# A two-layer encoder kernel: gates weighed two units sooner, scores scaled in place by the instruction that takes their extremum, queries turned with tables that hold gain and angle

## The chip, the cores and the metric

The kernel runs on one NeuronCore of a Trainium2 chip. The metric is the device time of one execution in microseconds (us). The kernel before has a median of 2119.84 us over three runs (2119.44 to 2119.92). The engines are called PE (TensorE, matrix products; PEld is its weight load), DVE (VectorE), ACT (ScalarE), POOL (GpSimd) and SP (SyncE, which here only issues DMAs).

## The reference, cut to what matters

The program is an encoder of two layers over 512 tokens of width 2048: gated grouped-query attention, then gated retention, each followed by a layer norm. The change touches the attention layer alone. There are 16 query heads of 128 elements in 4 groups; each group shares one key and value head.

```
def rms_norm(x, gain):
    y = x32 * lax.rsqrt(jnp.mean(x32 * x32, axis=-1, keepdims=True) + RMS_EPS)
    return (y * gain).astype(x.dtype)

def apply_rope(x, cos, sin):
    a, b, c, d = jnp.split(x32, 4, axis=-1)
    rot = jnp.concatenate([-b, a, -d, c], axis=-1)
    return x32 * cos + rot * sin
...
    q = apply_rope(rms_norm(q, q_gain), cos, sin) * (A_HEAD_DIM ** -0.5)
    k = apply_rope(rms_norm(k, k_gain), cos, sin)
...
        s = jnp.einsum('bkgqd,bskd->bkgqs', qb, k)
        p = jax.nn.softmax(s, axis=-1)
        return jnp.einsum('bkgqs,bskd->bkgqd', p, v)
...
    return (o * jax.nn.silu(g)) @ w_out
```

## The kernel before

**Products.** Every float32 product is made of three matmuls of split operands (`mm3`, L267 to L269): high by high, high by low, low by high. A weight chunk of 128 x 1024 is loaded as `raw`; ACT casts its high half `whi` and DVE subtracts to get the low half `wlo` (`split`, L116). Chunks are split two ahead of their use (`AHEAD = 2`) and loaded three further ahead. The projections are made by a seven-product scheme of 2 x 2 blocks, so DVE also adds `raw` to `raw` (L186, L188) and operand quarters `xf` to `xf` (L312 to L318).

**Order.** The instructions of PE run in the order of the program text. Those of the other engines are put in order by a scheduler, which goes by what is ready and, among ready ones, by where they stand in the text. Each engine then runs its own list strictly in order and waits at semaphores.

**Queries and keys.** When a tile of 128 tokens of a query or key projection is complete, `deliver_1` hands it to `rotate`, a generator whose pieces run one by one at chunk starts (`run_later`): square (ACT, L683), times gain (DVE, L684), sum of squares (L689), reciprocal root on POOL (L504, into `q_rs` for queries), then the rotation in halves (L700, L703, L706, two of each). A key is also scaled by its reciprocal root (L710); a query is not, its `q_rs` is applied to the scores. Three chunks later `put` transposes the tile on PE (`r_dst`, L521) and stores it in DRAM. A stretch of the const pool, `tabs`, holds the gains, cosines and sines.

**Attention.** `attention` walks through units. A unit is one head `h` of one query tile `t` of one group `g`: 64 units in two calls of 32, which share PE with products of the projection (`work.pump`). At step `u` PE makes the scores of unit `u` (`scores`, 128 x 512 in a PSUM bank `s`); DVE takes their negated maximum (L772); ACT multiplies it by `q_rs` (L773) and takes the exponential with `q_rs` as scale and that product as bias (L775), with the row sum in `sm`. At step `u` also unit `u - 2` is turned (`turn`: four transposes `tr<-ident,p` on PE, split into `pTh` by ACT and `pTl` by DVE), and for every second unit the two heads up to unit `u - 4` are multiplied with the values (`values`, into `o`). After the last head of a tile `weigh` divides the tile's gate by the sums: a reciprocal on DVE (L789, `rs`) and a product on POOL (L791, `gate<-gate,rs`). `close` then transposes that gate on PE (`tr<-ident,gate`), and the product of both becomes an operand of the output projection.

Gates, queries, keys and values come back from DRAM by DMAs that SP issues (L750 to L762). POOL issues the accumulating weight loads (L144) and the stores, in one list with its arithmetic.

Of the kernel before, what the change touches and what calls it, by code (L numbers as in the profile page):

```python
# [13 lines left out]
P = 128  # L14
# [38 lines left out]
def encoder_trunk_kernel(  # L53
# [52 lines left out]
    def v4(x):  # L106
        return x.rearrange("p (n d) -> p n d", d=P)
# [569 lines left out]
        for i in range(2):  # L677
            hook(a_in[3], ORDER[t + 3 * i], 1 + i, residual_1, t, i)

    def rotate(t, qk, src, g, put):  # L680

        sq, x = temp("r_sq"), src
        nc.scalar.activation(sq, src, AF.Square)  # L683
        nc.vector.scalar_tensor_tensor(  # L684
            out=v4(x), in0=v4(src), scalar=P ** -0.5 if qk == 0 else 1.0,
            in1=gains[:, qk].unsqueeze(1).broadcast_to([P, 4, P]), op0=ALU.mult, op1=ALU.mult)
# [3 lines left out]
        if qk == 0:  # L690
            rs = q_rs[:, g, t]
        else:
            rs = small("k_rs", 4)
        rsqrt(rs, ss, 1.0 / P, RMS_EPS)
        yield
        dst = temp("r_dst")
        xv, tv, dv = [m.rearrange("p (n h i d) -> p n h i d", n=4, h=2, i=2) for m in (x, sq, dst)]
        cb, sb = [m[:, t].unsqueeze(1).broadcast_to([P, 4, 2, 32]) for m in (cos, sin)]
        for i in range(2):
            nc.vector.tensor_tensor(out=tv[:, :, :, i], in0=xv[:, :, :, 1 - i], in1=sb, op=ALU.mult)  # L700
            if i:
                yield
            nc.vector.tensor_tensor(out=dv[:, :, :, i], in0=xv[:, :, :, i], in1=cb, op=ALU.mult)  # L703
            if not i:
                yield
            nc.vector.tensor_tensor(out=dv[:, :, :, i], in0=dv[:, :, :, i], in1=tv[:, :, :, i],  # L706
                                    op=ALU.subtract if i == 0 else ALU.add)
        yield
        if qk:
            nc.vector.tensor_tensor(out=v4(dst), in0=v4(dst), in1=rs.unsqueeze(2).broadcast_to([P, 4, P]), op=ALU.mult)  # L710
        soon(3, put, dst)

    def deliver_1(blk, nb, t, src, own):
        kind, g = A_COLS[a_in.index(blk)][nb]
        if kind in "vg":
            o = src if own else temp("gt")
        if kind == "v":
            if not own:
                nc.scalar.copy(o, src)
            nc.gpsimd.dma_start(out=vD[:, t], in_=o)  # L720
        elif kind == "g":
            if blk is a_in[-1]:
                e = temp("e")
                nc.scalar.activation(e, src, AF.Tanh, scale=0.5)
                nc.vector.scalar_tensor_tensor(out=o, in0=e, scalar=1.0, in1=src, op0=ALU.add, op1=ALU.mult)
            else:
                nc.scalar.activation(o, src, AF.Silu)
            nc.gpsimd.dma_start(out=gD[g][:, t], in_=o)
        else:
            def put(m):  # L730
                o = temp("qkT")
                nc.scalar.copy(o, transpose4(m))
                stored.add((kind, g, t))
                if kind == "q":
                    nc.gpsimd.dma_start(out=qD[g][:, t], in_=o)
                else:
                    nc.gpsimd.dma_start(out=kD[:, :, tcols(t)], in_=v4(o))

            turn_soon(lambda t, src: rotate(t, 0 if kind == "q" else 1, src, g, put), t, src, own)

    class Group:
        def __init__(self, g, op=None):
            self.g, self.op, self.q, self.gate, self.ogs, self.pT, self.sm = g, op, {}, {}, {}, {}, {}
# [20 lines left out]
        def scores(self, t, h):  # L764
            sb = bank("s")
            q = self.q[t]
            mm3(sb, [half(q, i)[:, tcols(h)] for i in range(2)], [half(self.k, i) for i in range(2)], True, True)
            if h == 0:
                self.sm[t] = small("sm", 4)
            rs = q_rs[:, self.g, t, h:h + 1]  # L770
            nmax = small("nmax")
            nc.vector.tensor_reduce(out=nmax, in_=sb, axis=AX.X, op=ALU.max, negate=True)  # L772
            nc.scalar.mul(nmax, nmax, rs)  # L773
            pt = temp("p")
            nc.scalar.activation(pt, sb, AF.Exp, scale=rs, bias=nmax, accum_out=self.sm[t][:, h:h + 1])  # L775
# [8 lines left out]
        def weigh(self, t):  # L784

            rs, sm = small("rs", 4), self.sm.pop(t)
            if ("g", self.g) in A_COLS[-1]:
                nc.vector.tensor_scalar_mul(sm, sm, 2.0)
            nc.vector.reciprocal(rs, sm)  # L789
            gt = self.gate.pop(t)  # L790
            nc.gpsimd.tensor_tensor(out=v4(gt), in0=v4(gt), in1=rs.unsqueeze(2).broadcast_to([P, 4, P]), op=ALU.mult)  # L791
            self.gt = gt

        def values(self, t, hh):

# [6 lines left out]

        def close(self, t):
            gT = temp("gT")
            nc.scalar.copy(gT, transpose4(self.gt))
            if self.op:
                nc.vector.tensor_tensor(out=self.op.quarter(t // 2, self.g % 2)[:, :, tcols(t % 2)],
                                        in0=v4(self.ob), in1=v4(gT), op=ALU.mult)
                if t == 1:
                    self.op.form(1 + self.g % 2)  # L810
                return
            if t % 2 == 0:
                self.ogs[t // 2] = x4("ogh"), x4("ogl")
            nc.vector.tensor_tensor(out=gT, in0=self.ob, in1=gT, op=ALU.mult)
            split(*[half(m, t % 2) for m in self.ogs[t // 2]], gT)
# [4 lines left out]
    def attention(gs, nxt, work, pace):  # L820
# [4 lines left out]
        for u in range(len(units) + LOOK + 2):  # L825
            each = pace(u)
            if u < len(units):
                g, t, h = units[u]
                n = after[g]
                if h == 1:  # L830
                    if t + 2 < NT:
                        g.load_q(t + 2)
                    elif n:
                        if t + 2 == NT:
                            n.load_kv()
                        n.load_q(t + 2 - NT)
                if h == 2:
                    g.load_gate(t)
                p[u] = g.scores(t, h)
            work.pump(each / 2)  # L840
            w = u - LOOK
            if 0 <= w < len(units):
                g, t, h = units[w]
                g.turn(t, h, p.pop(w))
            w = u - LOOK - 2
            if w >= 0 and w % 2:
                g, t, h = units[w]
                g.values(t, h // 2)
                if h == HPG - 1:
                    g.weigh(t)  # L850
            work.pump(each / 2)
            if w >= 0 and w % HPG == HPG - 1:
                g.close(t)
# [414 lines left out]
```

## Time and profile before

| | us |
|---|---|
| median of three runs | 2119.84 |
| the profiled execution, its own time | 2120.09 |
| its span, first to last instruction | 2118.3 |
| first attention call (first to last gate product on PE) | 369 to 463 |
| second attention call | 501 to 615 |
| PE busy over the span, modelled | 2094.6 |
| DVE busy | 1605.4 |
| ACT busy | 1141.3 |
| POOL busy | 427.9 |

In a row of a view by groups stand the line, the engine, the operation, `out<-in` by the program's names, shapes, the count, and behind the bar the busy time in us, the mean duration of one in ns, and the idle time ahead of them with what ended it. In a view by windows each engine has its busy us and, in brackets, its number of instructions, then the granted PE clock as a share of full speed, the share of DMA engines that are busy, and GB/s. In a timeline the columns are the start in us, the duration in us, the instruction, and in square brackets idle time before it with the releaser. DVE instructions that follow each other without a wait overlap a little: 128 x 512 ones of 0.68 us start 0.60 us apart.

### The profile page before, as it was taken

To read this page: it belongs to the slowest core of one execution; us is meant where nothing else is said; L and a number is where in the kernel's file an instruction comes from. 1 tells how busy PE (TensorE), PEld (TensorE's weight loads), DVE (VectorE), ACT (ScalarE), POOL (GpSimd) and SP (SyncE) were. 2 spreads that over 40 slices of the span, in tenths; PEclk is the share of its full clock that TensorE was granted. 3 is DMA by queue.
4 is the path that set the end of the run, shared out by engine and by line. 5 is a ranking of instruction groups with operands and counts; after the bars stand their busy time and mean duration, and the time that the engine had idled before them with its cause. 6 is when DMAs were issued, how large, how long until landed. Compare 5 with 4: busy or idle time off the path is not lost.

```text
span 2118.3 us, 26577 instructions
## 1 busy us (share of the span) xinstructions
PE 2094.6 (99%) x9708; PEld 1734.8 (82%) x9708; DVE 1605.4 (76%) x2129; ACT 1141.3 (54%) x1554; POOL 427.9 (20%) x501
## 2 busy tenths in 40 slices
PE   9999999998999999999999999999999999999997
PEld 7888887887888887888888888888888878888886
DVE  7888877888766788667787686666686887979767
ACT  6555556777742664454444444444455666656432
POOL 1145233122210112121111211111211122222100
PEclk9999999999999999999999999999999999999999
DMA  9776788456684658586686775576675578777762
GB/s 347 198 169 155 234 257 196 133 160 134 132 232 137 196 140 225 162 239 164 179 237 170 186 212 160 125 203 170 128 213 156 179 189 191 180 192 176 207 198 80
DMA packets 121395, 388.70 MB, mean 183 GB/s; under 512 B 14768, under 2 KB 17840, under 8 KB 121264
## 3 DMA queue, kind: packets, MB, share of 16 engines
q0 software_dynamic: 50176, 161.51, 36.7%
q1 hardware_dynamic: 70656, 224.58, 31.5%
q8 instruction: 76, 1.25, 0.2%
q10 hardware_dynamic: 432, 0.92, 0.1%
q14 instruction: 55, 0.45, 0.1%
HBM read 317.74 MB, written 69.21 MB: 183 GB/s over the span
## 4 chain that ended last, share of the span: by engine, by line
PE 82%; issue 7%; DVE 3%; DMA 3%; POOL 2%; ACT 1%; POOLq 0%; DVEq 0%; ACTq 0%
PE acc L268 23%; PE acc L269 23%; PE acc L267 23%; PE tr L521 3%; PE o L267 2%; PE o L269 2%; PE o L268 2%; PE s L267 1%; PE s L269 1%; PE s L268 1%; DVE wlo L116 1%; DMA raw<-in_wr_in_dram 1%; POOL raw L144 1%; DMA raw<-in_wa_in_dram 1%; ACT whi L116 1%
## 5 line engine op out<-in xcount | busy, mean ns | idle before, releaser
L116 DVE TENSOR_TENSOR wlo<-raw,whi 128x1024 fp32r<-128x1024 f32 (+1 forms) x610 | 742.5, 1219 | 365.4 <-ACT whi L116 360.2
L116 ACT CAST whi<-raw 128x1024 fp32r<-128x1024 f32 (+1 forms) x610 | 638.3, 1049 | 665.2 <-PE acc L269 514.1
L267 PE MATMUL acc<-whi,f 128*128 128x512 f32 x2352 | 928.4, 395 | 0.4 <-ACT whi L116 0.3
L268 PE MATMUL acc<-wlo,f 128*128 128x512 f32 x2352 | 919.2, 391 | 3.9 <-DVE wlo L116 3.7
L269 PE MATMUL acc<-whi,f 128*128 128x512 f32 x2352 | 918.7, 391 | 0.0
L268 PEld LDWEIGHTS acc<-wlo,f 128*128 128x128 f32 x2352 | 443.0, 188 | 95.9 <-DVE wlo L116 8.8
L269 PEld LDWEIGHTS acc<-whi,f 128*128 128x128 f32 x2352 | 442.2, 188 | 92.8
L267 PEld LDWEIGHTS acc<-whi,f 128*128 128x128 f32 x2352 | 442.9, 188 | 88.9 <-ACT whi L116 1.2
L144 POOL DMA_DIRECT2D raw<-in_wr_in_dram x100 | 88.0, 884 | 397.5 <-DVE wlo L116 265.5
L385 ACT COPY t<-acc 128x512 f32<-128x512 f32 x150 | 85.0, 587 | 39.7 <-PE acc L269 34.4
L186 DVE TENSOR_TENSOR raw<-raw,raw 128x1024 f32<-128x1024 f32 x84 | 102.2, 1222 | 2.2 <-DMA raw<-in_wa_in_dram 0.9
L504 POOL TENSOR_TENSOR rstd<-rs_e,neg_half 128x1 f32<-128x1 f32 x40 | 30.4, 760 | 280.8 <-DVE rs_e L503 211.8
L188 DVE TENSOR_TENSOR raw<-raw,raw 128x1024 f32<-128x1024 f32 x68 | 82.8, 1218 | 2.7 <-DMA raw<-in_wr_in_dram 2.7
L116 DVE TENSOR_TENSOR f<-xf,f 128x1024 fp32r<-128x1024 f32 (+2 forms) x59 | 68.6, 1165 | 8.1 <-ACT f L116 8.0
L144 POOL DMA_DIRECT2D yD<-t x48 | 43.1, 986 | 131.9 <-DVE t L396 47.9
L116 ACT CAST f<-xf 128x1024 fp32r<-128x1024 f32 (+2 forms) x59 | 59.1, 1005 | 18.2 <-DMA xf<-in_xq_dram 5.9
L144 POOL DMA_DIRECT2D raw<-in_wa_in_dram x48 | 42.3, 881 | 128.3 <-DVE wlo L116 100.4
L267 PE MATMUL acc<-whi,ogh 128*128 128x512 f32 x160 | 62.5, 390 | 0.0
L269 PE MATMUL acc<-whi,ogl 128*128 128x512 f32 x160 | 62.3, 390 | 0.0
L268 PE MATMUL acc<-wlo,ogh 128*128 128x512 f32 x160 | 62.3, 390 | 0.0
L1065 ACT ACTIVATE o<-o,nmr,rstd 128x512 f32<-128x512 f32 x32 | 24.9, 778 | 59.4 <-DVE nmr L515 59.4
L116 DVE TENSOR_TENSOR pTl<-tr,pTh 128x512 fp32r<-128x512 f32 x64 | 43.8, 687 | 10.4 <-ACT pTh L116 10.1
(191 smaller groups left out, 2409.0 us busy)
## 6 DMA issues: line engine op xcount, KB each, us to landing
raw<-in_wr_in_dram SPq DMA_DIRECT2D x156, 512.0 KB, 4.9
raw<-in_wr_in_dram POOLq DMA_DIRECT2D x100, 512.0 KB, 5.8
raw<-in_wa_in_dram SPq DMA_DIRECT2D x66, 512.0 KB, 6.1
raw<-in_wa_in_dram POOLq DMA_DIRECT2D x48, 512.0 KB, 7.4
raw<-in_wr_p_dram SPq DMA_DIRECT2D x36, 512.0 KB, 4.8
yD<-t POOLq DMA_DIRECT2D x48, 256.0 KB, 6.5
raw<-in_wr_p_dram POOLq DMA_DIRECT2D x24, 512.0 KB, 7.4
raw<-in_wa_o_dram SPq DMA_DIRECT2D x16, 512.0 KB, 4.7
```

The lines of the kernel that those rows point to most:

```text
L116: x, y = nc.scalar.copy(hi, src), nc.vector.tensor_sub(lo, src, hi.bitcast(F32))
L144: return nc.gpsimd.dma_start(out=x, in_=src, accum_op=ALU.add)
L186: nc.vector.tensor_add(v, v, g[3, c])
L188: x = nc.vector.tensor_add(v, v, g[2, c])
L267: nc.tensor.matmul(ps, sh, mh, start=start, stop=False, skip_group_check=go_on)
L268: nc.tensor.matmul(ps, sh, ml, start=False, stop=False, skip_group_check=go_on)
L269: nc.tensor.matmul(ps, sl, mh, start=False, stop=stop, skip_group_check=go_on)
L385: nc.scalar.copy(keep[p, t], bk[CHAIN[p]][t])
L504: nc.gpsimd.tensor_tensor(out=dst, in0=e[:, :n], in1=neg_half[:, :n], op=ALU.pow)
L521: nc.tensor.transpose(out=b[:, tcols(i)], in_=src[:, tcols(i)], identity=ident)
L1065: nc.scalar.activation(o, b, AF.Identity, scale=rstd, bias=nmr)
```

## The change

There are three edits, all in the attention layer.

1. **Scores.** The queries now come out negated. One DVE instruction reads the scores from PSUM, multiplies them by `q_rs`, writes them back to the same bank, and takes their minimum into `nmax`. It stands for the DVE reduction (L772) and the ACT product (L773). The exponential takes the constant scale -1 in place of `q_rs`.
2. **Queries.** `rotate` is split in two. `rotate_k` does for keys what was done. Once the last key tile has been turned, `query_tables` makes two tables of 128 x 512 out of gain (times minus the root of the head size), cosine and sine, and copies them over `tabs`. `rotate_q` multiplies the query with the first, its swapped halves with the second, and adds: four DVE instructions in place of seven, beside the sum of squares and its small follower. It ends two pieces sooner, so a query's `put` comes two chunks sooner.
3. **Gates.** `weigh` is called when the last head of a tile is turned, not when its values are multiplied: two units sooner. Since a second gate can now be ready before the first is closed, they are kept by tile.

```
-            nc.vector.tensor_reduce(out=nmax, in_=sb, axis=AX.X, op=ALU.max, negate=True)
-            nc.scalar.mul(nmax, nmax, rs)
+            nc.vector.tensor_scalar(sb, sb, rs, None, op0=ALU.mult, op1=ALU.min, accum_out=nmax)
             pt = temp("p")
-            nc.scalar.activation(pt, sb, AF.Exp, scale=rs, bias=nmax, accum_out=self.sm[t][:, h:h + 1])
+            nc.scalar.activation(pt, sb, AF.Exp, scale=-1.0, bias=nmax, accum_out=self.sm[t][:, h:h + 1])
...
                 g, t, h = units[w]
                 g.turn(t, h, p.pop(w))
+                if h == HPG - 1:
+                    g.weigh(t)
             w = u - LOOK - 2
             if w >= 0 and w % 2:
                 g, t, h = units[w]
                 g.values(t, h // 2)
-                if h == HPG - 1:
-                    g.weigh(t)
...
+    def query_tables():
+        gq, made = gains[:, 0], [temp("tab") for _ in range(2)]
+        nc.vector.tensor_scalar_mul(gq, gq, -P ** -0.5)
+        g2, views = gq.rearrange("p (h i d) -> p h i d", h=2, i=2), []
+        for m, by, j in ((made[0], cos, 0), (made[1], sin, 1)):
+            v = m.rearrange("p (t h i d) -> p t h i d", t=NT, h=2, i=2)
+            for i in range(2):
+                nc.vector.tensor_tensor(out=v[:, :, :, i], in0=by, in1=g2[:, :, i ^ j].unsqueeze(1).broadcast_to(
+                    [P, NT, 2, 32]), op=ALU.mult)
+            if j:
+                nc.vector.tensor_scalar_mul(v[:, :, :, 0], v[:, :, :, 0], -1.0)
+            yield
+        for i in range(2):
+            nc.scalar.copy(half(tabs, i), made[i])
+        yield
+
+    def rotate_q(t, src, g, put):
+        sq, dst = temp("r_sq"), temp("r_dst")
+        nc.scalar.activation(sq, src, AF.Square)
+        nc.vector.tensor_tensor(out=v4(dst), in0=v4(src), in1=cosq[:, t].unsqueeze(1).broadcast_to([P, 4, P]),
+                                op=ALU.mult)
+        yield
+        ss = small("r_ss", 4)
+        nc.vector.tensor_reduce(out=ss, in_=v4(sq), axis=AX.X, op=ALU.add)
+        rsqrt(q_rs[:, g, t], ss, 1.0 / P, RMS_EPS)
+        yield
...
+        for i in range(2):
+            nc.vector.tensor_tensor(out=tv[:, :, :, i], in0=xv[:, :, :, 1 - i], in1=sb[:, :, :, i], op=ALU.mult)
+        yield
+        nc.vector.tensor_add(dst, dst, sq)
+        soon(3, put, dst)
...
+        if t == NT - 1:
+            steps.insert(1, query_tables())
```

PE keeps the same instructions in the same order, but for the transposes of turned queries (`tr<-ident,r_dst`), which stand earlier. On the other engines the scheduler makes new lists up to the end of the attention layer; behind it they are the same.

The first place is DVE's list before, around the reciprocal `rs` of the first tile of the second attention call (the ninth of 16). `pTl` is the low half of turned probabilities, `nmax` the maximum of a unit's scores, `r_ss`, `r_sq` and `r_dst` belong to the turning of queries, `wlo`, `raw`, `xf` and `f` to the weights and operands of products.

```order
L186 TENSOR_TENSOR raw_4052<-raw_4052,raw_4390 128x1024
L700 TENSOR_TENSOR r_sq_4435<-t_2936,tabs 128x8x32
L703 TENSOR_TENSOR r_dst_4554<-t_2936,tabs 128x8x32
L116 TENSOR_TENSOR pTl_4561<-tr_4562,pTh_4560 128x4x128
L116 TENSOR_TENSOR wlo_4550<-raw_4052,whi_4549 128x1024
L772 TENSOR_REDUCE nmax_4576<-s_4572 128x1
L116 TENSOR_TENSOR pTl_4561<-tr_4587,pTh_4560 128x4x128
L789 RECIPROCAL rs_4606<-sm_4290 128x4
L116 TENSOR_TENSOR wlo_4614<-raw_4336,whi_4613 128x1024
L318 SCALAR_TENSOR_TENSOR xf_3192<-xf_3192,xf_4175 128x1024
L706 TENSOR_TENSOR r_dst_4554<-r_dst_4554,r_sq_4435 128x8x32
L700 TENSOR_TENSOR r_sq_4435<-t_2936,tabs 128x8x32
```

The same stretch of DVE's list in the changed kernel (its own line numbers: L806 is the new score instruction, L822 the reciprocal):

```order
L116 TENSOR_TENSOR f_4449<-xf_3785,f_4448 128x1024
L822 RECIPROCAL rs_4462<-sm_4249 128x4
L806 TENSOR_SCALAR s_4486,nmax_4490<-s_4486,q_rs 128x512
L186 TENSOR_TENSOR raw_4011<-raw_4011,raw_4342 128x1024
L116 TENSOR_TENSOR pTl_4507<-tr_4508,pTh_4506 128x4x128
L806 TENSOR_SCALAR s_4518,nmax_4522<-s_4518,q_rs 128x512
L116 TENSOR_TENSOR wlo_4499<-raw_4011,whi_4498 128x1024
L116 TENSOR_TENSOR pTl_4507<-tr_4532,pTh_4506 128x4x128
L318 SCALAR_TENSOR_TENSOR xf_3158<-xf_3158,xf_4135 128x1024
```

The reciprocal stood behind both score instructions and both `pTl` of these two units and now stands ahead of them, and no piece of the turning of queries is left in the stretch.

The second place is ACT's list at the first exponential of the first attention call; before:

```order
L116 CAST whi_2939<-raw_2641 128x1024
L773 ACTIVATE nmax_2929<-nmax_2929,q_rs 128x1
L775 ACT_TABLE_LOAD
L775 ACTIVATE p_2932,sm_2928<-s_2924,nmax_2929,q_rs 128x512
L385 COPY t_2934<-acc_2808 128x512
L385 COPY t_2936<-acc_2809 128x512
L773 ACTIVATE nmax_2959<-nmax_2959,q_rs 128x1
```

And in the changed kernel (L808 is the exponential):

```order
L116 CAST whi_2920<-raw_2634 128x1024
L808 ACT_TABLE_LOAD
L808 ACTIVATE p_2913,sm_2910<-s_2906,nmax_2911 128x512
L385 COPY t_2915<-acc_2810 128x512
L385 COPY t_2917<-acc_2811 128x512
L808 ACTIVATE p_2942,sm_2910<-s_2936,nmax_2940 128x512
```

The load of ACT's function table stood behind the product L773, which waits for DVE; that product is gone, and nothing that waits for DVE stands ahead of the load.

The third place is DVE's list in the changed kernel where the last key tile has been turned and the tables are made (`tab`, L690 and L693; the copies over `tabs` stand on ACT, between two casts `whi`); L703 to L713 turn the first query:

```order
L116 TENSOR_TENSOR wlo_1376<-raw_771,whi_1375 128x1024
L690 TENSOR_TENSOR tab_1388<-tabs 128x8x32
L690 TENSOR_TENSOR tab_1389<-tabs 128x8x32 x2
L693 TENSOR_SCALAR tab_1389<-tab_1389 128x8x32
L116 TENSOR_TENSOR wlo_1413<-raw_794,whi_1412 128x1024
L703 TENSOR_TENSOR r_dst_1419<-t_1102,tabs 128x512
L707 TENSOR_REDUCE r_ss_1438<-r_sq_1418 128x4
L503 TENSOR_SCALAR rs_e_1440<-r_ss_1438 128x4
L713 TENSOR_TENSOR r_sq_1418<-t_1102,tabs 128x8x32
L116 TENSOR_TENSOR wlo_1435<-raw_813,whi_1434 128x1024
```

Before, the first query's pieces stood between these `wlo`; now the making of the tables stands there and the query's pieces behind it.

More of the change, by code (lines that the diff above doesn't have):

```diff
@@ L678, in encoder_trunk_kernel @@
             hook(a_in[3], ORDER[t + 3 * i], 1 + i, residual_1, t, i)
-    def rotate(t, qk, src, g, put):
-        sq, x = temp("r_sq"), src
+    cosq, sinq = [half(tabs, i).rearrange("p (t e) -> p t e", t=NT) for i in range(2)]
+    def query_tables():
[15 more added lines that the diff above has]
+        sq, dst = temp("r_sq"), temp("r_dst")
         nc.scalar.activation(sq, src, AF.Square)
-        nc.vector.scalar_tensor_tensor(
-            out=v4(x), in0=v4(src), scalar=P ** -0.5 if qk == 0 else 1.0,
-            in1=gains[:, qk].unsqueeze(1).broadcast_to([P, 4, P]), op0=ALU.mult, op1=ALU.mult)
+        nc.vector.tensor_tensor(out=v4(dst), in0=v4(src), in1=cosq[:, t].unsqueeze(1).broadcast_to([P, 4, P]),
+                                op=ALU.mult)
         yield
@@ L689, in rotate, with rotate_k @@
         nc.vector.tensor_reduce(out=ss, in_=v4(sq), axis=AX.X, op=ALU.add)
[L690 to L693, printed above, removed]
+        rsqrt(q_rs[:, g, t], ss, 1.0 / P, RMS_EPS)
+        yield
+        xv, tv = [m.rearrange("p (n h i d) -> p n h i d", n=4, h=2, i=2) for m in (src, sq)]
+        sb = sinq[:, t].rearrange("p (h i d) -> p h i d", h=2, i=2).unsqueeze(1).broadcast_to([P, 4, 2, 2, 32])
+        for i in range(2):
[3 more added lines that the diff above has]
+        soon(3, put, dst)
+    def rotate_k(t, src, put):
+        sq, x = temp("r_sq"), src
+        nc.scalar.activation(sq, src, AF.Square)
+        nc.vector.tensor_tensor(out=v4(x), in0=v4(src), in1=gains[:, 1].unsqueeze(1).broadcast_to([P, 4, P]),
+                                op=ALU.mult)
+        yield
+        ss, rs = small("r_ss", 4), small("k_rs", 4)
+        nc.vector.tensor_reduce(out=ss, in_=v4(sq), axis=AX.X, op=ALU.add)
         rsqrt(rs, ss, 1.0 / P, RMS_EPS)
@@ L708, in rotate @@
         yield
-        if qk:
-            nc.vector.tensor_tensor(out=v4(dst), in0=v4(dst), in1=rs.unsqueeze(2).broadcast_to([P, 4, P]), op=ALU.mult)
+        nc.vector.tensor_tensor(out=v4(dst), in0=v4(dst), in1=rs.unsqueeze(2).broadcast_to([P, 4, P]), op=ALU.mult)
         soon(3, put, dst)
+        if t == NT - 1:
+            steps.insert(1, query_tables())
     def deliver_1(blk, nb, t, src, own):
@@ L737, in put @@
                     nc.gpsimd.dma_start(out=kD[:, :, tcols(t)], in_=v4(o))
-            turn_soon(lambda t, src: rotate(t, 0 if kind == "q" else 1, src, g, put), t, src, own)
+            turn_soon(lambda t, src: rotate_q(t, src, g, put) if kind == "q" else rotate_k(t, src, put), t, src, own)
     class Group:
         def __init__(self, g, op=None):
-            self.g, self.op, self.q, self.gate, self.ogs, self.pT, self.sm = g, op, {}, {}, {}, {}, {}
+            self.g, self.op, self.q, self.gate, self.ogs, self.pT, self.sm, self.gt = g, op, {}, {}, {}, {}, {}, {}
         def load_kv(self):
@@ L791, in weigh @@
             nc.gpsimd.tensor_tensor(out=v4(gt), in0=v4(gt), in1=rs.unsqueeze(2).broadcast_to([P, 4, P]), op=ALU.mult)
-            self.gt = gt
+            self.gt[t] = gt
         def values(self, t, hh):
@@ L804, in close @@
             gT = temp("gT")
-            nc.scalar.copy(gT, transpose4(self.gt))
+            nc.scalar.copy(gT, transpose4(self.gt.pop(t)))
             if self.op:
```

## The prediction

> **What bounds the kernel now.** I read first the page's engine rows, then what PE waited for, then the windows over the attention layer, then the places where PE stood.
>
> ```profile
> PE 2094.6 (99%) x9708; PEld 1734.8 (82%) x9708; DVE 1605.4 (76%) x2129; ACT 1141.3 (54%) x1554; POOL 427.9 (20%) x501
> PE tr L521 <- POOL gate L791: 3.9, 1, 3.9
> PE acc L268 <- DVE wlo L116: 3.7, 7, 1.2
> PE tr L521 <- DVE pTl L116: 1.9, 1, 1.9
> ```
>
> PE is busy for 2094.6 of 2118.3 us, so whatever the change does on other engines counts only where PE stands or runs at a lower clock. The change leaves PE's work as it is. The two longest single waits are both in the attention layer: one transpose of a gate (3.9 us, for POOL) and one of probabilities (1.9 us, for DVE). The windows show where PE loses time:
>
> ```profile
> 340.00:365.00 25.00, 23.90 (x118) 18.51 (x117) 19.19 (x26) 20.71 (x42) 7.47 (x9) 1.00 0.81 156
> 410.00:450.00 40.00, 40.00 (x236) 34.38 (x236) 34.51 (x56) 31.39 (x64) 6.46 (x7) 1.00 0.42 137
> 450.00:478.00 28.00, 28.00 (x158) 23.99 (x157) 21.58 (x32) 18.78 (x35) 5.68 (x7) 1.00 0.66 163
> 478.00:510.00 32.00, 25.99 (x127) 21.02 (x126) 27.78 (x40) 21.09 (x41) 9.70 (x8) 0.89 0.61 121
> 510.00:560.00 50.00, 49.88 (x286) 42.56 (x285) 40.32 (x59) 38.14 (x78) 12.68 (x15) 1.00 0.61 145
> 484.70:488.20 3.50, 3.50 (x15) 3.21 (x14) 3.46 (x5) 2.82 (x6) 1.77 (x2) 0.51 0.50 58
> 488.20:497.00 8.80, 8.80 (x51) 7.28 (x50) 8.80 (x14) 5.62 (x9) 2.52 (x3) 1.00 0.61 96
> 501.80:505.30 3.50, 3.50 (x10) 2.66 (x9) 2.54 (x4) 2.05 (x3) 0.73 (x2) 0.51 0.99 183
> ```
>
> The second column is PE. From 478 to 510 it is busy 25.99 of 32 us: 6.0 us idle. The two short windows show a granted clock of 0.51 for 3.5 us each, right behind the two waits; 3.5 x 0.49 is 1.7 us lost in each, 3.4 together. At the start of attention, 340 to 365, another 1.1 us is idle, and 0.1 from 510 to 560. So some **10.6 us** (6.0 + 3.4 + 1.1 + 0.1) stand within reach; the rest of PE's idle time lies at the start, the end and in layer 2, where every list is unchanged.
>
> **The wait of 1.9 us** is DVE's queue:
>
> ```profile
> 483.63 0.66 PE L521 MATMUL tr<-ident,p 128*128 128x128 f32 x4 [1.90 <-DVE pTl L116]
> 481.69 0.69 DVE L684 SCALAR_TENSOR_TENSOR t<-t,tabs 128x512 f32<-128x512 f32 x1
> 482.29 0.68 DVE L772 TENSOR_REDUCE nmax<-s 128x1 f32<-128x512 f32 x1
> 482.89 0.68 DVE L116 TENSOR_TENSOR pTl<-tr,pTh 128x512 fp32r<-128x512 f32 x1
> ```
>
> PE's transpose is let go by a `pTl` that frees a bank. Ahead of that `pTl` DVE works without a gap, and a piece of the turning of a query (L684) stands among it. DVE is full here: 8.80 of 8.80 us from 488.2 to 497.
>
> **The wait of 3.9 us** is POOL's:
>
> ```profile
> 497.14 0.18 DVE L789 RECIPROCAL rs<-sm 128x4 f32<-128x4 f32 x1
> 497.23 1.20 DVE L116 TENSOR_TENSOR wlo<-raw,whi 128x1024 fp32r<-128x1024 f32 x1
> 498.34 1.23 DVE L318 SCALAR_TENSOR_TENSOR xf<-xf,xf 128x1024 f32<-128x1024 f32 x1
> 497.47 3.67 POOL L791 TENSOR_TENSOR gate<-gate,rs 128x512 f32<-128x512 f32 x1
> L791 POOL TENSOR_TENSOR gate<-gate,rs x3: 1035/1042/3668, 497.5 to 519.3; 128x512 f32<-128x512 f32 x3
> 174.41 9.62 POOL L504 TENSOR_TENSOR q_rs<-rs_e,neg_half 128x4 f32<-128x4 f32 x1 [3.35 <-DVE rs_e L503]
> ```
>
> The reciprocal comes late in DVE's list (497.14), and the product that takes 1.04 us in its median takes 3.67 here, beside DVE instructions with two inputs in SBUF. Another POOL instruction, of four elements a row, took 9.62 us beside such a run.
>
> **Edit 3, the gate.** In the new list the reciprocal stands two units sooner, ahead of two score instructions and two `pTl`. Those are two score products, two transposes and products in between: PE spends some 7 us on two units (7 score instructions in the 25 us from 340 to 365, 12 in the 40 us from 410 to 450, so 3.3 to 3.6 us a unit). The gate needs 1.0 to 3.7 us; a single stretch of DVE work as long as that cannot make it late. So the 3.9 us go, and with them the slow stretch behind them, 1.7 us. Nothing else is issued by this edit; on POOL the accumulating load queued behind the product is waited for chunks later. For the other 15 gates PE does not wait now, and gets nothing.
>
> [...]
>
> **Edit 2, the queries.** The rows of the turning:
>
> ```profile
> L684 DVE SCALAR_TENSOR_TENSOR t<-t,tabs 128x512 f32<-128x512 f32 x20 | 13.7, 685 | 0.4 <-ACT r_sq L683 0.2
> L700 DVE TENSOR_TENSOR r_sq<-t,tabs 128x256 f32<-128x256 f32 x40 | 16.8, 440 | 0.0
> L703 DVE TENSOR_TENSOR r_dst<-t,tabs 128x256 f32<-128x256 f32 x40 | 16.3, 418 | 0.0
> L706 DVE TENSOR_TENSOR r_dst<-r_dst,r_sq 128x256 f32<-128x256 f32 x40 | 16.4, 419 | 0.1
> L952 DVE TENSOR_TENSOR res<-res,ln_bias 128x512 f32<-128x512 f32 x16 | 10.7, 687 | 0.2
> 150.00:200.00 50.00, 49.67 (x229) 40.77 (x228) 42.32 (x77) 28.84 (x39) 28.21 (x18) 1.00 0.56 134
> ```
>
> Before: 685 + 2 x (440 + 418 + 419) = 3239 ns a query tile. After, two full ones like L952 and two like L700: 2 x 687 + 2 x 440 = 2254. That is 0.985 us less, 15.8 us over 16 tiles, nearly all beside PE work. What counts is where the pieces go. Counting both lists at the spacing of their starts (0.60 and 0.33 us), 5.4 us of turning stood behind the 33rd score instruction, in the stretch up to 500 us; now none does. Some 3.8 us more than before stand between the 21st and 33rd, about 412 to 453 us. The `pTl` that was 1.9 us late loses the pieces queued ahead of it in the 15 us before (L684, two L703, two L706: 0.60 + 4 x 0.33 = 1.9 us).
>
> The tables cost four instructions like L700 and two smaller ones (each under 440 ns), at most 2.6 us of DVE once, and two ACT copies of 128 x 512, under 0.71 us each by the L453 row below. They stand in the stretch 150 to 200, where DVE has 7.7 us free and the first query's pieces come later in exchange. The cover is that weights are split two chunks ahead: 229 matmuls in 50 us make a chunk of 12 last 2.6 us, so 5.2 us. I cost them at 0. If ACT's copies, waiting for DVE, held the next cast `whi` beyond the lead, it would be 1 to 2 us.
>
> **Edit 1, the scores.**
>
> ```profile
> L772 DVE TENSOR_REDUCE nmax<-s 128x1 f32<-128x512 f32 x64 | 43.7, 685 | 8.8 <-PE s L269 8.6
> L910 DVE TENSOR_SCALAR y<-y,mv,rstd 128x512 f32<-128x512 f32 x8 | 4.1, 539 | 0.0
> L1135 DVE SCALAR_TENSOR_TENSOR z<-y,k_rs,ln_gain 128x512 f32<-128x512 f32 x16 | 11.8, 747 | 0.0
> L423 DVE DVE_READ_ACCUMULATOR y<-y,acc 128x1 f32 x16 | 1.3, 82 | 0.0
> L773 ACT ACTIVATE nmax<-nmax,q_rs 128x1 f32<-128x1 f32 x64 | 18.9, 295 | 17.1 <-DVE nmax L772 17.0
> L775 ACT ACTIVATE p<-s,nmax,q_rs 128x512 f32<-128x512 f32 x64 | 50.0, 781 | 1.3
> L453 ACT ACTIVATE sq<-y,nmax 128x512 f32<-128x512 f32 x16 | 11.4, 713 | 32.5 <-DVE nmax L460 32.4
> L912 ACT ACTIVATE y<-y,nmr,rstd 128x512 f32<-128x512 f32 x8 | 6.1, 809 | 11.1 <-DVE nmr L515 11.1
> 347.29 1.28 ACT L775 ACT_TABLE_LOAD   x1
> ```
>
> No row shows a DVE instruction that writes PSUM, nor this one with an accumulator. The low end is 539 ns (L910, the same operation within SBUF); the high end is 685 + 539 = 1224, a reduction and a scaling one after the other. I take 747 + 82 = 829: one element a step as L772 goes from PSUM, one per-partition scalar as in L1135, and the reading of the accumulator. That is 144 ns more on DVE for each of 64 units, 9.2 us, beside other work.
>
> On ACT each unit loses L773 (295 ns), and the exponential one per-partition operand: 809 - 713 = 96 ns. ACT gets 25 us back (64 x 0.39). The path from scores to probabilities gets shorter by 295 + 96 - 144, a quarter of a us a unit. At the first unit the table load (1.28 us) need no longer wait for DVE. PE's idle 1.1 us at 340 to 365 stand while ACT and DVE start the first units; I take 0.7 of them as gone.
>
> **The sum.** Gate wait 3.9; `pTl` wait 1.9, less three score instructions ahead of it at 0.145, so 1.5; the rest of the 6.0 idle, 0.2; slow clock 3.4; start 0.7. Together 9.7 us. From the profiled execution, 2120.09 (span 2118.3 and 1.8 around it), that leaves 2110.4. It is 0.25 above the median, so against the median **2110.1 us**.
>
> [...]
>
> **The rivals.**
>
> *DVE stays late at 481.* For it: the forecast's 829 ns is unseen, and with 3.8 us of turning moved in and 12 x 0.145, DVE's 34.5 us from 410 to 450 become 40.0 of 40. At 1224 ns another 12 x 0.4 = 4.8 us are added there, about the lead of 5.2, so the next stretch starts late and the 1.9 us and their 1.7 stay. Against: 5.4 us leave that next stretch. It gives 2110.1 + 3.6 = 2113.7.
>
> *The gate still waits on POOL.* For it: the 9.62 us. If DVE runs two-input work for the whole 7 us behind the reciprocal, the gate ends as late as before relative to PE and 3.9 + 1.7 stay: 2115.7. Against: the two score instructions and two `pTl` in between read PSUM.
>
> *No effect.* Gate and `pTl` waits go, but PE waits next for something else as long, say the `wlo` behind them (3.7 us in seven waits now, 1.2 the longest), or the scheduler's lists put the lateness elsewhere. Against: from 510 on DVE has 9.7 of 50 us free. About 2119.
>
> *Slower.* The write back to PSUM is dear, and DVE becomes the bound of the attention calls. The four windows from 410 to 560 hold 36 score instructions (12, 5, 7, 12), and DVE is free there for 5.5 + 6.4 + 4.2 + 9.7 = 25.8 us, plus 1.6 of turning that leaves on balance and a lead of 5.2: 32.6 us. At 1.6 us (starts 1.52 apart, 0.92 more than now) 36 of them take 33.1, and the room is used up; every further 0.1 us costs 3.6. The gate and the start still gain 3.9 + 1.7 + 0.7 = 6.3, so it decides at about 1.7 us, with the two slow stretches back. At 1.9 us: 10.8 + 3.4 - 6.3 = 7.9, 2128. Against: L772 takes 685 ns from PSUM, and L952 takes 687 within SBUF, so the place of an operand costs nothing in reading.
>
> **How the numbers follow.** Forecast 0.66, DVE late 0.14, gate still late 0.06, no effect 0.08, slower 0.06. A run tells 0.2% (4.2 us) from no change: faster is below 2115.6. Faster takes the forecast and DVE late, and a little of the gate's: 0.81; same 0.13; slower 0.06. The range: the low end takes all 10.6 and half of the `wlo` waits left over, about 2107, and 2106.5 with the low price of the score; the high end takes in both partial rivals, 2116.5.
>
> **What would show it.** In the profile of the changed kernel: no wait of PE for POOL's gate; none over 1 us for `pTl`; no clock of 0.51 between 470 and 520; PE idle under 1 us from 478 to 510; the score instruction near 0.75 plus 0.08 us; the exponential near 0.69; ACT's busy time some 23 us less; DVE's some 4 less (15.8 + 0 - 9.2 - 2.6). The prediction falls if the score instruction takes over 1.2 us, if PE waits for `wlo` from 410 to 450, or if a clock of 0.51 comes without a wait before it.

## The result, and the profile after

The kernel after takes **2109.61 us** in the median of four runs (2109.24 to 2111.01), the kernel before 2119.88 beside it (2119.44 to 2121.83): a ratio of 0.9951, 95% interval 0.9934 to 0.9968. 2110.1 was forecast. The profiled execution took 2111.01 us, its span is 2109.2 us against 2118.3.

The page's engine rows of the changed kernel, then what PE waited for over the whole span (us in all, times, longest):

```profile
PE 2090.0 (99%) x9708; PEld 1732.4 (82%) x9708; DVE 1600.9 (76%) x2151; ACT 1121.3 (53%) x1492; POOL 411.5 (20%) x501
PE acc L268 <- DVE wlo L116: 5.0, 8, 1.1
PE acc L267 <- ACT whi L116: 0.8, 1, 0.8
```

The waits for POOL's gate and for `pTl` are gone. Those for split weights (`wlo`, `whi`) have grown from 3.7 + 0.3 to 5.0 + 0.8 us. The windows of the changed kernel (second column PE, the ratio near the end the granted clock):

```profile
410.00:450.00 40.00, 40.00 (x238) 34.23 (x237) 36.81 (x68) 28.07 (x53) 7.67 (x8) 1.00 0.43 137
478.00:510.00 32.00, 31.55 (x179) 26.83 (x178) 31.60 (x49) 25.38 (x48) 8.41 (x10) 1.00 0.67 139
330.00:365.00 35.00, 32.81 (x158) 26.56 (x157) 26.32 (x38) 22.95 (x39) 6.82 (x8) 1.00 0.86 194
```

And the last of them in the kernel before:

```profile
330.00:365.00 35.00, 33.90 (x164) 26.64 (x163) 26.10 (x34) 25.48 (x48) 7.47 (x9) 1.00 0.85 187
```

From 478 to 510 PE's idle time falls from 6.0 to 0.45 us, and the clock stays at 1.00. From 330 to 365, where 0.7 us less was forecast, it rises from 1.10 to 2.19.

The gate that PE waited for, on the queues of POOL and DVE of the changed kernel (start, duration, instruction, idle time before it):

```profile
489.47 0.17 DVE L822 RECIPROCAL rs<-sm 128x4 f32<-128x4 f32 x1
489.56 0.73 DVE L806 TENSOR_SCALAR_CACHE_REDUCE s<-s,q_rs 128x512 f32<-128x512 f32 x1
490.21 0.14 DVE L806 DVE_READ_ACCUMULATOR s<-s,q_rs 128x1 f32 x1
490.21 1.76 DVE L186 TENSOR_TENSOR raw<-raw,raw 128x1024 f32<-128x1024 f32 x1
489.79 1.09 POOL L824 TENSOR_TENSOR gate<-gate,rs 128x512 f32<-128x512 f32 x1
```

The reciprocal comes 7.7 us sooner than before (489.47 against 497.14; PE itself is some 3 us ahead by then), the product takes 1.09 us in place of 3.67, behind a score instruction that reads PSUM, and it is done at 490.88, while PE transposes the gate at 493.99. The wait has turned into 3.1 us of room. What does run beside it, the addition at 490.21, takes 1.76 us; the same L186 takes 1.23 at 338.59 (a row further down), with no arithmetic on POOL beside it.

### The profile page after: what moved, and what is told of

It is laid out like the page before. It is cut to its first block, busy times and chain, and to the rows that moved or that the text cites. A ratio compares the mean times of both kernels' runs of the same rounds, so it can differ in the third digit from the quotient of the medians.

```text
span 2109.2 us, 26590 instructions
## 1 busy us (share of the span) xinstructions
PE 2090.0 (99%) x9708; PEld 1732.4 (82%) x9708; DVE 1600.9 (76%) x2151; ACT 1121.3 (53%) x1492; POOL 411.5 (20%) x501
## 4 chain that ended last, share of the span: by engine, by line
PE 91%; DMA 3%; DVE 3%; issue 1%; POOL 1%; ACT 1%; POOLq 0%; DVEq 0%; ACTq 0%
PE acc L268 26%; PE acc L269 26%; PE acc L267 26%; PE tr L521 3%; PE o L267 2%; PE o L268 2%; PE o L269 2%; PE s L267 1%; PE s L269 1%; PE s L268 1%; DMA raw<-in_wr_in_dram 1%; DMA raw<-in_wa_in_dram 1%; DVE wlo L116 1%; DMA xf<-in_xq_dram 1%; ACT whi L116 1%
## 5 line engine op out<-in xcount | busy, mean ns | idle before, releaser
L186 DVE TENSOR_TENSOR raw<-raw,raw 128x1024 f32<-128x1024 f32 x84 | 102.9, 1229 | 3.8 <-DMA raw<-in_wa_in_dram 2.0
L808 ACT ACTIVATE p<-s,nmax 128x512 f32<-128x512 f32 x64 | 44.1, 689 | 21.4 <-DVE s L806 18.0
```

The lines of the kernel that those rows point to most:

```text
L186: nc.vector.tensor_add(v, v, g[3, c])
L808: nc.scalar.activation(pt, sb, AF.Exp, scale=-1.0, bias=nmax, accum_out=self.sm[t][:, h:h + 1])
```

## The experiments

In the captions, edit 1 is the score instruction, edit 2 the queries' tables, edit 3 the earlier weighing. The kernels were timed in three series, each on another chip, with the kernel before beside each: 2119.14 us in the first (31 runs, 2113.91 to 2122.43), 2119.25 in the second (24 runs, 2114.24 to 2122.47), 2116.97 in the third (17 runs, 2113.74 to 2119.79). The last two profiles of the kernel before are single runs on a fourth chip, with one more run of 2117.46 us beside them. Ratios are to the kernel before of the same series, with a 95% interval; they differ by up to 0.0006 from the quotients of the medians given.

**One edit at a time.** Edit 3 alone:

```
+                if h == HPG - 1:
+                    g.weigh(t)
             w = u - LOOK - 2
...
-                if h == HPG - 1:
-                    g.weigh(t)
```

> The kernel before with the third edit alone (weigh called two units sooner). Theory A, one wait to one edit: PE's 3.9 us wait for POOL's gate near 500 us goes and the slow-clock stretch behind it (1.7 us) too, while the 1.9 us wait for pTl near 482 and its slow stretch stay: 2119.9 - 5.6 = 2114.3. Rival B, the gate is late because DVE is full of the turning of queries: the reciprocal stands earlier in the list but POOL is still held, over 2 us of the wait stay, 2117 or more.

2115.32 us (2113.78 to 2119.36, 10 runs), ratio 0.9986 [0.9977, 0.9996]. Edit 2 alone (tables, `rotate_q`, as in the change):

> The kernel before with the second edit alone (queries turned with tables; gain positive, scores and weigh as before). Theory A: the wait for pTl and its slow stretch go (1.9 + 1.7), the gate's wait and its slow stretch stay: 2116.3. Rival B, an emptied DVE is all that the gate needed: both waits and both slow stretches go, 2110.5, and the third edit is idle.

2113.28 us (2111.51 to 2115.39, 10 runs), ratio 0.9977 [0.9967, 0.9986]. Edit 1 alone (the exponential with scale -1 as in the change, the queries negated in the old turning):

```
-            nc.vector.tensor_reduce(out=nmax, in_=sb, axis=AX.X, op=ALU.max, negate=True)
-            nc.scalar.mul(nmax, nmax, rs)
+            nc.vector.tensor_scalar(sb, sb, rs, None, op0=ALU.mult, op1=ALU.min, accum_out=nmax)
...
```

> The kernel before with the first edit alone (scores scaled in place; queries negated in the old turning). Theory A: both big waits stay; the score instruction costs DVE some 0.1 us a unit and the start of attention gains at most 0.7: 2119 to 2121. Rival C, the shorter path from scores to probabilities is what removed the wait for pTl: 3.6 us less, 2116.3.

2114.96 us (2113.18 to 2119.81, 10 runs), ratio 0.9986 [0.9976, 0.9997]. What PE waited for from 478 to 516 us, in the kernel with edit 3 alone, then edit 2, then edit 1:

```profile
PE tr L521 <- DVE pTl L116: 1.8, 1, 1.8
PE tr L521 <- issue: 0.9, 1, 0.9
```

```profile
PE tr L521 <- POOL gate L825: 1.9, 1, 1.9
```

```profile
PE tr L521 <- POOL gate L790: 3.0, 2, 2.2
PE s L267 <- DVE pTl L116: 1.6, 1, 1.6
PE tr L521 <- DVE pTl L116: 1.2, 1, 1.2
```

So edit 3 takes away the wait for POOL and leaves the one for `pTl`, with a stretch of half clock behind it. Edit 2 takes away those for `pTl` and leaves half of POOL's (1.9 of 3.9 us; the product takes 1.82 us in place of 3.67), with one stretch of half clock; its time lies between the two theories. The row `issue` is the gate's transpose, which still stands 0.9 us with edit 3 alone. POOL's product is done at 493.02 us there, and the transpose starts at 497.82, 0.10 us behind the end of a `pTl`: by these times it waits for DVE and no longer for POOL. The time of that kernel is 1.0 us over theory A. But for these remainders, each edit does in this stretch what the prediction gave it.

Edit 1 alone leaves both, 5.8 us in all. That it still gained 4 us was not expected. In its profile the 5.8 us are spread over four waits, behind none of which the clock was halved (3.4 us less than in the first profile of before), and the start of attention has 0.25 us of idle. Over all ten runs, though, its mean granted clock is 0.9977, that of the kernel before 0.9973, which is worth some 0.8 us. Where most of the 4 us comes from in the other runs is not shown.

```profile
330.00:365.00 35.00, 34.75 (x175) 28.69 (x174) 28.06 (x44) 24.13 (x42) 7.46 (x9) 1.00 0.88 201
```

**Two edits at a time.** Without edit 3 (`weigh` back behind `values`):

> The changed kernel with weigh called where it was before (first and second edits stay). Theory A: the gate's wait comes back with its slow stretch, 3.9 + 1.7 us: 2115.2. Rival B: DVE is empty enough there, the wait does not come back, 2109.6 to 2110.5.

2114.45 us (2111.50 to 2116.35, 10 runs), ratio 0.9978 [0.9969, 0.9988]. One wait is left between 478 and 510, without a stretch of half clock behind it, so theory A holds for the wait alone: the reciprocal comes late again (493.98), and the product takes 1.82 us.

```profile
PE tr L521 <- POOL gate L824: 2.4, 1, 2.4
494.34 1.82 POOL L824 TENSOR_TENSOR gate<-gate,rs 128x512 f32<-128x512 f32 x1
```

Without edit 1 (maximum on DVE, its scaling on ACT):

> The changed kernel without its first edit: VectorE takes the extremum of the raw scores alone again and ScalarE scales it, so only the queries' tables and the earlier weighing are in. Theory A, by which the end is set by the gate wait, the wait of the 33rd score and the slow clock, and the first edit only clears work off ScalarE: the run with the queries' edit alone had one gate wait of 2.0 us and one slow stretch (1.7 us) left, both of which the earlier weighing removes, so 2113.3 - 3.7 = 2109.6 us, within 1.5 us of the changed kernel run beside it, and no slow clock between 478 and 510 us. Theory B, by which the first edit has a gain of its own (it gave 4 us alone): 2112 to 2114 us, with waits for ScalarE's p where the changed kernel has none.

2112.13 us (2110.92 to 2114.00, 8 runs), ratio 0.9970 [0.9960, 0.9980]. Without edit 2 (`rotate` for queries as before):

> The changed kernel without its second edit: queries are turned as before, so 13 pieces of turning stand behind the 33rd score again. Theory A: the waits for pTl between 478 and 490 us come back (the run with the first edit alone showed 1.4 and 1.8 us there) and the gate waits (2.4 and 0.9 us in that run) do not: 2115.0 - 3.3 = 2111.7 us, between 2111 and 2113, with a slow stretch only if 2 us or more of the waits fall in one window of the clock. Theory B, by which the order of the turning is of no consequence once the first edit has lightened ScalarE: within 1 us of the changed kernel, and no wait over 0.7 us between 478 and 510 us.

2112.18 us (2110.20 to 2114.06, 7 runs), ratio 0.9967 [0.9956, 0.9978]. The changed kernel in the same series:

> The changed kernel itself, beside the three that leave out a part, and beside more executions of the kernel before. Theory A, by which no pause of TensorE in it is long enough for a slow clock: its runs lie within 1.5 us of their median of about 2109.6 us, while those of the kernel before spread by 5 us or more, as a slow stretch of 1.7 us does or does not follow a pause. Theory B, by which the spread of the kernel before belongs to the chip and not to its pauses: the changed kernel spreads by 5 us too.

2111.72 us (2109.72 to 2114.20, 8 runs), ratio 0.9968 [0.9957, 0.9979]. Its runs spread by 4.5 us: less than the 8.2 of the kernel before beside it, more than the 3 that theory A allowed; neither theory is met.

Without edit 1 there is no wait over 0.5 us from 478 to 510 and the time is 0.4 us from the changed kernel's, as theory A had it; the 2109.6 us themselves were missed by 2.5. The time lies in theory B's range too, but the waits for `p` that B asked for are not there. Without edit 2 the time fits both theories, and the waits decide for A: those for `pTl` are back (the row `issue` is the gate's transpose again, 0.11 us behind the end of a `pTl`):

```profile
PE s L267 <- DVE pTl L116: 1.6, 1, 1.6
PE tr L521 <- DVE pTl L116: 1.2, 1, 1.2
PE tr L521 <- issue: 1.0, 1, 1.0
478.00:510.00 32.00, 27.94 (x154) 22.90 (x153) 31.46 (x52) 21.33 (x39) 8.96 (x10) 1.00 0.63 118
330.00:365.00 35.00, 34.19 (x169) 28.03 (x168) 28.06 (x44) 24.46 (x42) 7.47 (x9) 1.00 0.89 201
```

That kernel loses 4.06 us at 478 to 510, 3.6 more than the changed one, and is but 0.5 us slower in the median. A part of that it has back at 330 to 365: 0.81 us of idle, where the changed kernel beside it had 2.58:

```profile
330.00:365.00 35.00, 32.42 (x156) 26.13 (x155) 26.82 (x39) 22.36 (x37) 6.82 (x8) 1.00 0.84 194
```

Singly, in the first series, edits 3, 2 and 1 gain 3.8, 5.9 and 4.2 us, 13.9 in all; together they gain 10.3 us in the first pair of kernels, 7.5 in the second series and 5.6 in the third. No series had both. But in the second, leaving out edit 1 or edit 2 costs only 0.4 or 0.5 us. The edits share one stretch and its slow clock, and can't gain it twice.

**The start of attention.** With edit 2 a query is ready sooner: its store to DRAM is issued at 332.66 us (before: 342.50), and the gate's load, queued behind the next query's on SP, at 334.18 (before: 341.10). In POOL's and SP's lists after:

```profile
332.66 0.56 POOL L769 DMA_DIRECT2D qD<-qkT  x1 [5.43 <-ACT t L385]
334.18 0.43 SPq L796 DMA_DIRECT2D gate<-gD  x1
```

Both then lie among transfers that keep the DMA engines busy: their share from 320 to 341 us is counted at 1.04 (280 GB/s), before at 0.91 (227 GB/s). An accumulating load of weights, issued by POOL at 325.46 before and 326.36 after, lands later; in the view of DMA issues (KB each, us to landing), before and after:

```profile
raw<-in_wa_in_dram POOLq DMA_DIRECT2D x1, 512.0 KB, 12.6
```

```profile
raw<-in_wa_in_dram POOLq DMA_DIRECT2D x1, 512.0 KB, 14.7
```

ACT stands until it lands, DVE behind ACT, and PE behind both. Before, ACT stood for that load as well (3.73 us), but went on at 338.16 us and not at 341.12. The queues of ACT, DVE and PE after:

```profile
341.12 1.04 ACT L116 CAST whi<-raw 128x1024 fp32r<-128x1024 f32 x1 [3.30 <-DMA raw<-in_wa_in_dram]
338.59 1.23 DVE L186 TENSOR_TENSOR raw<-raw,raw 128x1024 f32<-128x1024 f32 x1
342.19 1.23 DVE L116 TENSOR_TENSOR wlo<-raw,whi 128x1024 fp32r<-128x1024 f32 x1 [1.77 <-ACT whi L116]
342.21 0.49 PE L267 MATMUL acc<-whi,f 128*128 128x512 f32 x1 [0.81 <-ACT whi L116]
343.47 0.50 PE L268 MATMUL acc<-wlo,f 128*128 128x512 f32 x1 [0.77 <-DVE wlo L116]
```

The durations of matmuls are modelled and overlap, so the idle column understates short waits. Counted from start to start (the last two rows stand 1.26 us apart, a pair without a wait 0.23: a wait of 1.03), the waits at 337 to 343 us cost 2.8 us after and 0.5 before. In the same count five waits at 349 to 361 us, four of them for ACT's `p`, are gone, 1.6 us in all.

Two kernels put one of the two transfers back. The store later:

```
         nc.vector.tensor_add(dst, dst, sq)
-        soon(3, put, dst)
+        soon(5, put, dst)
```

> The changed kernel with the turned queries' stores put back two chunks later, where they stood before the change, and nothing else. Theory A, by which the 2.8 us of waits at 337 to 343 us come from the one store more that the second edit put into the saturated stretch of transfers at 320 to 345 us: the accumulating load of raw issued at about 326 us lands in under 13.5 us (14.7 in the changed kernel), the waits there fall to 1.6 us or less, and the time to 2108.0 to 2108.9 us, 1 us under the changed kernel. Theory B, by which the burst is as long without that store: the landing stays at 14 us or more and the time within 0.5 us of the changed kernel.

2113.17 us (2112.31 to 2114.89, 10 runs), ratio 0.9973 [0.9964, 0.9982], 1.45 us over the changed kernel: a miss in time. The load landed in 13.6 us (under 13.5 was expected) and the idle time from 330 to 365 fell to 1.65 us, but the later `put` also moves the transposes of `r_dst` and pieces on ACT and DVE, and a new wait stands where there was none. How the one leads to the other was not followed.

```profile
330.00:365.00 35.00, 33.35 (x161) 26.81 (x160) 26.20 (x38) 23.02 (x40) 6.83 (x8) 1.00 0.83 190
490.13 0.50 PE L267 MATMUL s<-k,q 128*128 128x512 f32 x1 [1.44 <-ACT p L808]
```

The first gate's load of each attention call later, and no other line moved:

```
-                if h == 2:
+                if h == 2 and u > 2:
                     g.load_gate(t)
+                if u == 5:
+                    gs[0].load_gate(0)
```

> The changed kernel with one load moved: the gate of the first tile of a group of units is fetched behind the load of the fourth tile's queries (three units later), so that its 256 KB no longer lie in the saturated stretch of transfers before 343 us (in the changed kernel it is issued at 334.2 us, in the kernel before at 341.1). Theory A, by which every transfer in that stretch pushes back the accumulating load of raw: 256 KB at some 400 GB/s are 0.65 us, so that load, issued at about 326.5 us, lands in 14.0 to 14.5 us where it took 14.7 and 15.2, the three waits at 337 to 343 us come to 2.2 to 2.7 us (2.8 and 3.3 in the two profiles of the changed kernel), and the time falls by 0.6 us. Theory B, by which the gate's load only fills what the accumulating load leaves free: landing and waits as in the changed kernel, and the time within 0.3 us of it.

2110.74 us (2107.86 to 2115.26, 10 runs), ratio 0.9972 [0.9963, 0.9981]. The measure beside it:

> The changed kernel again, as the measure for the kernel with the later load. Its time is expected within 1 us of the 2111.7 us of the previous series, with three waits of 2.8 to 3.3 us in all at 337 to 343 us, and no slow clock before the end unless two of them fall into one window of the clock with 2.1 us of idle in all.

2111.40 us (2109.95 to 2113.45, 8 runs), ratio 0.9974 [0.9964, 0.9985]. Its profile has a stretch of half clock behind a window with 1.82 us of idle, where 2.1 had been asked for. With the later gate the load of weights lands in 13.4 us where 14.8 are taken beside it, and the idle time from 330 to 365 is 1.22 against 2.34 us; the kernel with the later gate, then the changed one beside it:

```profile
raw<-in_wa_in_dram POOLq DMA_DIRECT2D x1, 512.0 KB, 13.4
330.00:365.00 35.00, 33.78 (x164) 27.64 (x163) 26.04 (x39) 23.14 (x40) 6.82 (x8) 1.00 0.84 181
```

```profile
raw<-in_wa_in_dram POOLq DMA_DIRECT2D x1, 512.0 KB, 14.8
330.00:365.00 35.00, 32.66 (x148) 26.19 (x147) 25.65 (x37) 22.01 (x37) 6.83 (x8) 0.95 0.83 183
```

The median is 0.66 us lower, as theory A expected, but by less than the runs spread: that it is faster than the changed kernel is not settled. Nor is the cause. Over all profiles the same load lands in 12.5 to 14.3 us in the six executions without the two transfers in the stretch, and in 13.2 to 15.2 in the six with both. The ranges overlap, and something else goes with the landing: how close together POOL issues this load and the three of its kind ahead of it, from 317 to 327 us, before the gate's load is issued at all. With both transfers it lands in 14.7 to 15.2 us where the four issues lie within 6.7 to 7.3 us, and in 13.2 and 13.4 where they take 8.3 and 8.2 (without edit 3, and edit 2 alone). Without them it lands in 12.5 to 13.4 us at 6.6 to 7.5, and in 14.3 at 5.6. So at like spacing the two transfers go with 1 to 3 us. The kernel with the later gate has a spacing of 8.3 us and lands as the two with 8.3 and 8.2 do, which load the gate early: that its load lands sooner is not shown to be the gate's doing. No run changed the spacing alone.

PE's idle time overlaps too. The kernel without edit 3 has both transfers in the stretch and 1.00 us of idle, and the last profile of the kernel before (below) has neither and 2.28:

```profile
330.00:365.00 35.00, 34.00 (x166) 27.90 (x165) 26.50 (x38) 23.61 (x40) 6.81 (x8) 1.00 0.83 188
```

```profile
330.00:365.00 35.00, 32.72 (x156) 25.29 (x155) 27.00 (x35) 24.50 (x46) 7.48 (x9) 1.00 0.86 193
```

So the two transfers are a likely cause and not a proven one.

**The kernel before, two more profiles.**

> The kernel before itself, profiled once more, since its runs spread by 6 to 8.5 us in each series while the one profile of it had both waits and two slow stretches. Theory A, by which the spread comes from its two waits: the wait for pTl near 481 us and the one for POOL's gate near 497 us are there again, the gate's between 1.5 and 4 us as POOL's product takes 1 to 3.7 us, and a window of 3.41 us is followed by one at half clock if PE is busy in it for 1.6 us or less, and not if it is busy for 1.8 us or more; the time follows from these, at 1.7 us a slow window. Theory B, by which the spread lies elsewhere: both waits and both slow stretches are as in the first profile, and the time differs through waits outside 478 to 510 us.

> As the run before it: a second look at the same kernel on the same chip. Theory A: the sum of idle PE time and slow clock between 478 and 510 us (9.4 us in the first profile) differs between the three profiles by 1.7 us or more, and the spans differ by as much. Theory B: that sum is 9.4 us within 0.5 us in all three.

They took 2119.84 and 2116.41 us, spans of 2118.1 and 2114.6. The waits come back, but not their sizes. Windows of the first, where the stretch of half clock lasts two windows, and of the second:

```profile
478.00:510.00 32.00, 24.68 (x120) 19.79 (x119) 26.60 (x38) 19.93 (x39) 9.71 (x8) 0.89 0.62 118
496.02:499.43 3.41, 0.46 (x2) 0.02 (x1) 3.40 (x6) 2.45 (x6) 3.28 (x2) 1.00 0.63 74
499.43:502.85 3.42, 2.47 (x8) 2.18 (x9) 0.69 (x1) 1.32 (x2) 2.29 (x3) 0.50 1.05 190
```

```profile
478.00:510.00 32.00, 26.87 (x147) 21.86 (x146) 31.11 (x46) 23.80 (x46) 8.77 (x9) 1.00 0.61 118
```

Idle time and slow clock from 478 to 510 come to 6.0 + 3.4, 7.3 + 2.9 (half of the 5.9 us that PE was busy at half clock) and 5.1 + 0 us in three executions of one kernel. The second run's theory A holds between the third and the others: 4.3 us less than the first there, 1.2 us more idle time from 330 to 365, and a span 3.7 us shorter. Between the first two it does not: the sum is 0.8 us larger and the span 0.2 shorter, so something outside makes up for the rest. Of the first run's theories neither holds whole. Its gate wait is 3.9 us again, but there is no half clock behind the wait for `pTl`, and the second slow window behind the gate's follows one in which PE was busy for 2.47 us, at half clock, where theory A let 1.8 suffice.

## Why the prediction was right, and where it was not

**The gate** (3.9 us): right. Both ends were found: edit 3 alone removes the wait for POOL (0.9 us of the transpose's remain, for `pTl` by their times), and without edit 3 it stands at 2.4 us. The room behind the reciprocal was put at some 7 us less 1.0 to 3.7 for the product; 4.5 us passed from reciprocal to transpose, 3.1 of them to spare.

**The `pTl` wait** (1.5 us): right in cause. It goes with edit 2 and comes back without it. The 0.145 us by which each score instruction was to slow it were too much: on DVE's queue the next instruction starts together with the reading of the accumulator, 0.67 us after the score instruction (0.60 for the maximum before):

```profile
420.90 0.75 DVE L806 TENSOR_SCALAR_CACHE_REDUCE s<-s,q_rs 128x512 f32<-128x512 f32 x1
421.57 0.14 DVE L806 DVE_READ_ACCUMULATOR s<-s,q_rs 128x1 f32 x1
421.57 0.68 DVE L116 TENSOR_TENSOR pTl<-tr,pTh 128x512 fp32r<-128x512 f32 x1
```

So 0.07 us a unit and not 0.144. By durations the guess was low, 752 + 142 = 894 ns for 829:

```profile
L806 DVE TENSOR_SCALAR_CACHE_REDUCE s<-s,q_rs 128x512 f32<-128x512 f32 x64 | 48.1, 752 | 6.8 <-PE s L269 6.6
L806 DVE DVE_READ_ACCUMULATOR s<-s,q_rs 128x1 f32 x64 | 9.1, 142 | 0.0
L808 ACT ACTIVATE p<-s,nmax 128x512 f32<-128x512 f32 x64 | 44.1, 689 | 21.4 <-DVE s L806 18.0
L713 DVE TENSOR_TENSOR r_sq<-t,tabs 128x256 f32<-128x256 f32 x32 | 14.0, 474 | 0.0
```

The exponential is at 689 ns for 685; the halves of the turning at 474 for 440. DVE's busy time falls by 4.5 us (4.0 forecast), ACT's by 20.0 (23 forecast). With 36.81 of 40 us busy from 410 to 450, DVE is not late behind it: the first rival fell. So did the slower one, whose point was 1.7 us for a score instruction, and the one by which the gate would still wait on POOL. Of the case without effect a little came true: the waits for split weights grew, in one place. The tables, held at 0, cost PE nothing; the window that takes them in has 49.66 us of PE where it had 49.67:

```profile
150.00:200.00 50.00, 49.66 (x231) 40.77 (x229) 44.25 (x78) 30.07 (x41) 28.15 (x20) 1.00 0.53 134
```

**The slow clock** (3.4 us): right in the profiled pair, but its size differs between executions of one kernel: 3.4, 2.9 and 0 us from 478 to 510 in the three of the kernel before. The prediction booked both stretches in full. Edit 1 alone lost them with both waits standing, and the changed kernel itself, with no wait over 0.7 us from 478 to 510, had one from 343.4 us in one of three executions, behind the waits at 340 to 343:

```profile
340.01:343.42 3.41, 1.59 (x6) 0.78 (x5) 1.50 (x2) 2.57 (x5) 0.00 (x0) 1.00 0.26 99
343.42:346.83 3.41, 3.41 (x9) 2.63 (x9) 3.33 (x5) 1.93 (x3) 0.86 (x1) 0.50 0.30 71
```

That is a part of why the gain differs: 10.3, 7.5 and 5.6 us. Over all runs the mean granted clock rose from 0.9970 to 0.9979 in the second series, just under 2 us of 2119, and in the third it went from 0.9976 to 0.9974, so the clock gave nothing there. What else differs between the series, the sizes of the waits or the chips, was not tried.

**The start** (0.7 us): here a step failed. "I take 0.7 of them as gone" holds for edit 1 alone, where the idle time from 330 to 365 fell from 1.10 to 0.25 us. It left out what the prediction's own counting asks for, the DMAs of the step that edit 2 moves: with the query ready sooner, its store and a gate's load go sooner too, and the idle time rose to 2.19 us, with 2.58 and 2.34 in the other two profiles. That these two transfers are what raised it is likely and not proven, as shown above. In that column the step is 1.8 us off. Counted from start to start, 1.6 us of short waits went, more than was forecast, and 2.3 us came at 337 to 343, so 0.7 was added where 0.7 was to go.

**The sum** came out at 9.1 us of span for 9.7 (2118.3 to 2109.2), in that count: 4.1 for the gate's wait, 2.1 for the `pTl` wait where 1.5 was booked, 3.4 for the clock, less the 0.7 of the start; the other 0.2 are small gaps elsewhere. One term with the wrong sign was hidden by two that were larger than booked and one that happened to be whole.

## What to carry to other kernels

Edits that clear the same stretch don't add up: two that gained 4.2 and 5.9 us alone were, in another series, worth 0.4 and 0.5 us beside the others, so a change is to be priced against the stretch as the others leave it. A step made ready sooner takes its transfers with it, and each queue they are put in belongs to the sum. Before a difference of a few us is explained from one profile, take a second one of the same kernel: here 3.7 us lay between two executions of the kernel before.

## What the runs showed of the hardware

In the first profile of the kernel before, two stretches of 3.41 us at a clock of 0.50 begin at 484.75 and 501.81 us, 17.06 us or five times their length apart. Cut into windows of 3.41 us in step with such stretches, the windows of the attention layer at full clock and right ahead of half clock had PE busy for 0.62 and 1.51 us in that profile, 0.46 in the second of the same kernel, 1.53 with edit 2 alone, 1.57 with edit 3 alone, 1.59 in the third of the changed kernel and 1.77 without edit 1: PE stood through none of the seven. Of the windows with the longest waits that were not followed by half clock, the lowest had 1.77 us (the later store), then 1.79 and 1.84 (edit 1 alone) and 1.97 (the second profile of the kernel before). The two at 1.77 us, without edit 1 (followed) and with the later store (not followed):

```profile
340.37:343.78 3.41, 1.77 (x7) 0.93 (x6) 1.59 (x2) 2.67 (x5) 0.00 (x0) 1.00 0.30 114
```

```profile
487.13:490.54 3.41, 1.77 (x9) 1.25 (x10) 3.41 (x6) 1.83 (x4) 1.84 (x2) 1.00 0.67 102
```

At the end of the changed kernel's span, where its last products run, a window with 1.67 us was not followed by half clock either:

```profile
2096.53:2099.94 3.41, 1.67 (x8) 1.05 (x6) 1.94 (x10) 2.94 (x8) 0.00 (x0) 1.00 0.01 2
2099.94:2103.35 3.41, 0.00 (x0) 0.00 (x0) 2.97 (x9) 0.00 (x0) 0.92 (x1) 1.00 0.00 0
```

So PE's modelled busy time does not part the two kinds sharply. The 2 and 2.1 us of idle in one window that two of the expectations asked for were the author's estimates and are not borne out: 1.64 us (3.41 less 1.77) was once enough. Nor does the length of a wait tell: the one of 1.8 us with edit 3 alone was followed by a stretch of half clock, 1.7 us lost, the one of 2.4 us without edit 3 was not. What decides between them no run shows.
